# Transposed attention scores as four pairs of 64-row products, with the row maxima in the same shape

## The chip, the cores and the metric

The kernel runs on one core of a Trainium2 chip. The metric is the device time of one execution in microseconds. Before the change it is 2519.74 us (median of three runs, 2518.32 to 2525.74).

The core has a matrix engine (TensorE, PE in the profile, its weight loads listed as PEld), a vector engine (VectorE, DVE), an engine for activations (ScalarE, ACT), a general engine (GpSimd, POOL) and a queue for transfers (SyncE, SP). Operands lie in the on-chip memory of 128 partitions. Products go to PSUM, which has eight banks of 512 float32 per partition here.

## The reference

A two-layer encoder over 1024 tokens of width 1024, in float32. Layer 0 mixes tokens by attention, layer 1 by pooling; each layer then attends to 256 memory tokens and runs a gated network with a width-3 convolution. The change touches layer 0's attention and the start of what follows it. With 16 query heads and 4 key heads of width 64 it computes

```
q = rope(rmsnorm(q)) * 64 ** -0.5 ; k = rope(rmsnorm(k))
scores = einsum('bkgqd,bksd->bkgqs', q, k)      # 1024 x 1024 for each of 16 heads
p = softmax(scores)                             # over the keys
o = einsum('bkgqs,bksd->bkgqd', p, v)
x = x + o @ w_o
```

The gains of the normalisations are large, so the scores are too, and the exponentials need the row maxima taken off first.

## The kernel before

**Precision.** Products run on operands in a reduced float32 form. Each operand is split into a high and a low part, and a product is the sum of high x high, high x low and low x high (lines 759 to 761, the helper for all large products). The high part is made on ScalarE (line 672), the low part on VectorE (line 675).

**Stages.** `attention` has two stages with a planner each. The first (94 to 184 us of it concern this text) makes keys, values and queries from the normalised tokens, tile of 128 tokens by tile, in the order of the list `QKV`. The second is the attention loop, from 183.9 to 544 us. Then `run` multiplies by `w_o`, adds the residual rows `X` and goes on.

**The planner.** A `Plan` collects steps with an engine, an estimated time, what they read and write and which pool of buffers they take from. TensorE's steps keep the order in which they are added. Those of the other engines are ordered by due times, which are worked back from the TensorE steps that need them; `late` sets a due time by hand, so many microseconds behind TensorE's planned clock. `plan.run()` plays this forward and emits the instructions. Outside of the planners the framework orders the instructions. An instruction that waits blocks its engine's queue.

**Layout of q and k.** Queries and keys are kept transposed: the 64 numbers of a head on partitions, tokens along the row. `K[0]` holds the high part of a key head twice, on partitions 0 to 63 and 64 to 127. `K[1]` holds the low part on partitions 0 to 63 and a row of ones on partition 64 (`plan_ones`, line 1133). A block of `Q` holds one query head: its high part on one half of the partitions and its low part on the other, and which half is which changes with the head's parity.

**Groups.** The loop runs over 16 groups, a group being a pair of query heads (x = 0, 1) with one half of the queries (512), and in a group over eight tiles of 128 keys. Two key tiles make a step, four steps a group.

**Scores** (`plan_scores`, lines 1222 and 1224) come transposed, keys on partitions, queries along the row, since the values' product needs them so. For one head and key tile that is a product of 128 rows (high keys with both parts of the queries) and one of 65 (low keys with a copy of the high queries, and the row of ones with a row of negated maxima). The result lies in one PSUM bank (`pT`, three of them), and ScalarE makes its exponential of 512 columns (line 1232) into a half of a tile `pt` (six tiles).

**Maxima** (`peaks`, line 789; `biggest`, line 795) come from the same scores, not transposed and in the high parts alone: queries on partitions, 64 rows, two heads on the two halves of the partitions. The pair fills a tile `pA` of two banks (two such tiles), and one VectorE reduction of 1024 columns gives two columns of `nm`. After eight of them `joined` (line 802) makes eight columns, and `shift` sends them as eight small transfers (line 814) into the row beside the copy of the high queries, which two more transfers bring (line 810). The place of this copy is a ring of four halves of storage slots. The maxima of a group are made during the group before it, and for the first group during the first stage (items `S` of `QKV`).

**Values and sums** (`plan_values`, line 1260; `plan_sum`, line 1293): a step's values product stands one step behind its scores, in full float32, two heads on the two column halves. VectorE adds the two exponentials of each step (line 1267), POOL adds these up over the group (line 1270), and a product with ones sums over the partitions. The sums go by small transfers through a reciprocal (line 1306) and back, POOL scales the result (line 1320), and it is split in high (ScalarE) and low (VectorE) parts for `w_o`.

Of the kernel before, what the change touches and what calls it, by code (L numbers as in the profile page):

```python
# [10 lines left out]
F32 = mybir.dt.float32  # L11
# [32 lines left out]
         for it in ([q, ("S", n // 3)] if n % 3 == 2 else [q])),  # L44
       ("V", 4), ("V", 5), ("V", 6), ("V", 7))
# [588 lines left out]
class Kernel:  # L634
# [140 lines left out]
    def attention(self):  # L775
# [6 lines left out]

        def peaks(G, n, S):

            half, m = GROUPS[G]
            q, t, kh = R.v(Q[m // 2, half], 4), n // 2, n % 2
            for x in range(2):
                rows = slice(x * HD, (x + 1) * HD)
                nc.tensor.matmul(S[:, x * 512:(x + 1) * 512], q[rows, m % 2 * 2 + x, t * P:(t + 1) * P],  # L789
                                 R.v(K[0][kh], 4)[rows, m // 2], start=True, stop=True)  # L790

        def biggest(G, n, S):
            if n == 0:
                NM[G] = self.stat(16, "nm")
            nc.vector.tensor_reduce(NM[G][:, 2 * n:2 * n + 2], S.rearrange("p (x k) -> p x k", x=2), axis=AX.X, op=OP.max,  # L795
                                    negate=True)
# [8 lines left out]
        def shift(G, h):  # L805

            half, m = GROUPS[G]
            q, qm = R.v(Q[m // 2, half], 4), R.hv(h).bitcast(F32)
            for x in range(2):
                nc.sync.dma_start(out=qm[:HD, x * 512:(x + 1) * 512],  # L810
                                  in_=q[x * HD:(x + 1) * HD, m % 2 * 2 + x].bitcast(F32))
            nm = NM.pop(G)
            for i in range(8):
                nc.sync.dma_start(out=qm[HD:HD + 1, i * P:(i + 1) * P], in_=nm[:, i:i + 1].bitcast(F32))  # L814

        with tc.tile_pool(name="qk", bufs=1, reuse_waits="tile") as qk, self.psum("psq", 1, 6) as self.ps:
# [222 lines left out]
            def plan_k(t, b):  # L1039
# [4 lines left out]
                def view(h):  # L1044
                    return R.hv(h)[:, :768].rearrange("p (h i c) -> p h i c", h=4, i=3)
# [5 lines left out]
                def low():  # L1051
                    kst = view(at[half])
                    nc.vector.tensor_tensor(out=kst[:, :, 2], in0=q3(), in1=kst[:, :, 0].bitcast(F32), op=OP.subtract)
                plan.add("copy", 650, high, [qn], [half], [("half", half)], [qn])
                plan.add("add", 350, low, [qn, half], [half], uses=[qn, half])
# [3 lines left out]
            def plan_turn_k(t):  # L1059
                half = ("kst", t)  # L1060
                for i in range(2):
                    b = ("kturned", t, i)

                    def turn(i=i, b=b):
                        kst = R.hv(at[half])[:, :768].rearrange("p (h i c) -> p h i c", h=4, i=3)
                        p = at[b] = self.psB().rearrange("p (a b) -> p a b", a=4)
                        for h in range(4):
                            src = kst[:, h, 2] if i else kst[:, h, :2].rearrange("p a b -> p (a b)")
# [1298 lines left out]
```

## Time and profile before

| what | value |
|---|---|
| median of three runs | 2519.74 us |
| profiled execution | 2520.43 us, its span 2518.7 us |
| PE / PEld / DVE / ACT / POOL busy | 99% / 78% / 77% / 49% / 14% of the span |
| attention loop | 183.9 to 544 us of the span |
| granted clock over the whole span | 0.993 |

A row of a group reads: line, engine, operation, output<-inputs with shapes, xcount | busy us, mean ns of one | idle us of the engine just before, and who ended it. A row of the timeline reads: start in us from the span's start, duration in us, engine, line, operation, xcount of merged instructions, and in brackets the idle time before with its releaser. Ends of products are modelled and overlap with what follows, so starts are the better measure. A granted clock of 1.00 is the full clock of TensorE.

### The profile page before, as it was taken

Reading aid. Unit: us, or ns where it says so; the run is one execution under the profiler, and the core shown is the slowest. Engines: PE = TensorE matmul, PEld = TensorE weight load, DVE = VectorE, ACT = ScalarE, POOL = GpSimd, SP = SyncE. Lnnn points to the kernel's source line nnn. Section 1 sums busy time; section 2 is a strip of 40 time slices with the busy share of each in tenths; the row PEclk is TensorE's granted clock in tenths of the full one; section 3 lists DMA queues with packets and bytes.
Section 4 is the critical chain, followed back from the end, with each engine's and each line's share of the span. In section 5 each row is a group of like instructions: output and inputs, shape, how many; then the busy total and the mean of one; then the engine's idle time right before and its main releaser. Section 6 shows DMA issues by size and latency. Waiting matters only on the chain.

```text
span 2518.7 us, 33712 instructions
## 1 busy us (share of the span) xinstructions
PE 2485.2 (99%) x12302; PEld 1962.5 (78%) x12302; DVE 1936.9 (77%) x2645; ACT 1229.3 (49%) x2070; POOL 355.6 (14%) x407
## 2 busy tenths in 40 slices
PE   9999999999999999999999999999999999999998
PEld 9984434357899888888888888889888888888887
DVE  7887877853886479888879775887559988888875
ACT  6544545542546346554556443655436554554542
POOL 5663433330102000000000002102000000000001
PEclk9998999999999999999999999999999999999999
DMA  4310111142487123432448663289223423337852
GB/s 162 92 26 14 26 26 26 36 145 73 155 299 237 48 80 103 124 105 87 122 145 280 191 215 94 103 280 331 84 76 97 123 86 109 111 103 243 283 193 96
DMA packets 334171, 329.11 MB, mean 131 GB/s; under 512 B 32941, under 2 KB 264733, under 8 KB 334005
## 3 DMA queue, kind: packets, MB, share of 16 engines
q1 hardware_dynamic: 334005, 326.95, 40.7%
q8 instruction: 97, 1.59, 0.3%
q14 instruction: 69, 0.57, 0.1%
HBM read 235.10 MB, written 82.64 MB: 126 GB/s over the span
## 4 chain that ended last, share of the span: by engine, by line
PE 82%; DVE 8%; issue 3%; DMA 3%; SPq 2%; POOL 0%; ACT 0%; POOLq 0%; DVEq 0%; ACTq 0%
PE pB L759 22%; PE pB L761 22%; PE pB L760 22%; PE pA L761 3%; PE pA L759 3%; PE pA L760 3%; DVE nm L795 2%; SPq L814 2%; DVE R L675 2%; DVE scr L1267 2%; PE pO L1260 1%; PE pT L1222 1%; PE pB L328 1%; PE pT L1224 1%; PE pA L789 1%
## 5 line engine op out<-in xcount | busy, mean ns | idle before, releaser
L759 PE MATMUL pB<-R,R 128*128 128x512 f32 (+1 forms) x2732 | 1016.1, 372 | 2.3 <-ACT R L672 0.9
L761 PE MATMUL pB<-R,R 128*128 128x512 f32 (+1 forms) x2728 | 1008.5, 370 | 2.2 <-DVE R L675 2.1
L760 PE MATMUL pB<-R,R 128*128 128x512 f32 (+1 forms) x2732 | 1009.7, 370 | 0.2 <-DVE R L675 0.2
L759 PEld LDWEIGHTS pB<-R,R 128*128 128x128 f32 x2732 | 515.5, 189 | 93.7 <-ACT R L672 2.1
L761 PEld LDWEIGHTS pB<-R,R 128*128 128x128 f32 x2728 | 514.6, 189 | 90.2 <-DVE R L675 3.9
L760 PEld LDWEIGHTS pB<-R,R 128*128 128x128 f32 x2732 | 515.6, 189 | 86.5 <-DVE R L675 1.2
L672 ACT ACTIVATE R<-scr 128x512 fp32r<-128x512 f32 (+3 forms) x376 | 272.9, 753 | 235.8 <-DMA scr<-Gs 59.3
L675 DVE TENSOR_TENSOR R<-scr,R 128x512 fp32r<-128x512 f32 (+3 forms) x364 | 321.4, 911 | 29.7 <-ACT R L672 29.1
L675 DVE TENSOR_TENSOR R<-X,R 128x512 fp32r<-128x512 f32 x374 | 252.1, 685 | 67.5 <-ACT R L672 66.8
L672 ACT ACTIVATE R<-X 128x512 fp32r<-128x512 f32 x374 | 231.8, 630 | 133.7 <-PE pB L760 66.6
L732 POOL TENSOR_SCALAR ms<-ss 128x1 f32<-128x1 f32 (+2 forms) x97 | 31.0, 320 | 1652.2 <-ACT R L740 1282.9
L1232 ACT ACTIVATE pt<-pT 128x512 f32<-128x512 f32 x256 | 148.8, 599 | 151.3 <-PE pT L1224 149.6
L442 ACT COPY scr<-pB 128x512 f32<-128x512 f32 x156 | 91.0, 584 | 180.3 <-PE pB L761 173.2
L795 DVE TENSOR_REDUCE nm<-pA 128x2 f32<-128x1024 f32 x128 | 150.6, 1211 | 27.7 <-PE pA L789 27.6
L1942 DVE TENSOR_TENSOR X<-pB,X 128x512 f32<-128x512 f32 (+1 forms) x145 | 99.3, 686 | 82.5 <-PE pB L761 81.2
L759 PE MATMUL pA<-R,R 128*128 128x512 f32 (+1 forms) x420 | 150.7, 359 | 0.0
L761 PE MATMUL pA<-R,R 128*128 128x512 f32 (+1 forms) x420 | 150.3, 358 | 0.0
L760 PE MATMUL pA<-R,R 128*128 128x512 f32 (+1 forms) x420 | 150.0, 357 | 0.0
L1270 POOL TENSOR_TENSOR scr<-scr 128x1024 f32<-128x1024 f32 x46 | 115.2, 2504 | 191.9 <-DVE scr L1267 191.9
L1260 PE MATMUL pO<-pt,V 128*64 128x512 f32 x512 | 127.1, 619 | 0.0
L1222 PE MATMUL pT<-R,R 128*128 128x512 f32 x256 | 121.9, 476 | 0.0
L1222 PEld LDWEIGHTS pT<-R,R 128*128 128x128 f32 x256 | 48.7, 190 | 85.9 <-issue 53.5
(182 smaller groups left out, 3065.1 us busy)
## 6 DMA issues: line engine op xcount, KB each, us to landing
X<-in_ffn_w_up SPq DMA_DIRECT2D x82, 512.0 KB
Gs<-X SPq DMA_DIRECT2D x105, 256.0 KB
scr<-in_ffn_w_down SPq DMA_DIRECT2D x45, 512.0 KB
scr<-Gs SPq DMA_DIRECT2D x35, 512.0 KB
scr<-in_xattn_w_kv SPq DMA_DIRECT2D x32, 512.0 KB
scr<-Gs SPq DMA_DIRECT2D x42, 384.0 KB
scr<-in_attn_w_qkv SPq DMA_DIRECT2D x22, 512.0 KB
Wt<-scr SPq DMA_DIRECT2D x44, 256.0 KB
```

What stands on the lines that cost most here:

```text
L442: self.nc.scalar.copy(out, p)
L672: self.nc.scalar.activation(hi, src, AF.Copy)
L675: self.nc.vector.tensor_tensor(out=lo, in0=src, in1=hi.bitcast(F32), op=OP.subtract)
L759: mm(out, ah, bh, start=start, stop=False)
L760: mm(out, ah, bl, start=False, stop=False)
L761: mm(out, al, bh, start=False, stop=stop)
L795: nc.vector.tensor_reduce(NM[G][:, 2 * n:2 * n + 2], S.rearrange("p (x k) -> p x k", x=2), axis=AX.X, op=OP.max, negate=True)
L1222: nc.tensor.matmul(T[b], R.v(K[0][kt // 4], 4)[:, m // 2, cols], R.v(Q[m // 2, half], 4)[:, m % 2 * 2 + x], start=True, stop=False)
L1232: nc.scalar.activation(E[G, kt][:, x * 512:(x + 1) * 512], T.pop(b), AF.Exp)
L1260: nc.tensor.matmul(O[G][x * HD:(x + 1) * HD], V32[:, kt, m // 2], E[G, kt][:, x * 512:(x + 1) * 512], start=kt == 0, stop=kt == NT - 1)
L1270: nc.gpsimd.tensor_tensor(out=acc[G, 0], in0=acc[G, 0], in1=acc.pop((G, d)), op=OP.add)
L1942: nc.vector.tensor_tensor(out=x, in0=banks[b][:, c], in1=x, op=OP.add)
```

## The change

Layout: a block of `Q` now holds one part of two query heads, one on each half of the partitions; the next block holds the other part. `K[1]` holds the low part of a key head on both halves, made by a fourth column block in the staging of the keys. Queries are no longer copied for the shift.

Scores: a key tile of both heads goes into one PSUM tile of two banks (two such tiles), as four pairs of 64-row products, the two heads on the two halves: high keys with high queries, high keys with low queries, low keys with high queries, and a block `one` (zeros, and ones on partitions 0 and 64) with a block that holds the negated maxima on partitions 0 and 64. The last pair is a step of its own, which alone waits for the shift. One exponential covers both heads. The blocks of the shift lie in one slot, zeroed once in the first stage; `shift` sends the eight small transfers alone.

Maxima: the two heads go to single banks (`pS`, three, which the column sums share) and are reduced apart, 512 columns each. Ahead of and behind the scores of a step stands one pair of maxima, and in the first four steps a third between them. In the first stage the last two pairs stand among the last values products, and the last reduction, the join and the transfers get due times.

POOL: of a group's four steps the last is not added on VectorE but by two POOL additions that read the exponentials. The low parts of the result are made on POOL.

Residual rows: the six tiles `pt` are placed first in their pool, and the tiles `X` are placed in the order 1, 3, 0, 2, 4, 6, 5, 7 over them and what follows.

```diff
-         for it in ([q, ("S", n // 3)] if n % 3 == 2 else [q])),
-       ("V", 4), ("V", 5), ("V", 6), ("V", 7))
+         for it in ([q, ("S", n // 4)] if n % 4 == 1 else [q])),
+       ("S", 6), ("V", 4), ("S", 7), ("V", 5), ("V", 6), ("V", 7))
...
+        def rows(x):
+            return slice(x * HD, (x + 1) * HD)
...
-                rows = slice(x * HD, (x + 1) * HD)
-                nc.tensor.matmul(S[:, x * 512:(x + 1) * 512], q[rows, m % 2 * 2 + x, t * P:(t + 1) * P],
-                                 R.v(K[0][kh], 4)[rows, m // 2], start=True, stop=True)
+                nc.tensor.matmul(S[x], q[rows(x), m % 2 * 2, t * P:(t + 1) * P], R.v(K[0][kh], 4)[rows(x), m // 2],
+                                 start=True, stop=True)
...
-        def shift(G, h):
...
-            for x in range(2):
-                nc.sync.dma_start(out=qm[:HD, x * 512:(x + 1) * 512],
-                                  in_=q[x * HD:(x + 1) * HD, m % 2 * 2 + x].bitcast(F32))
-            nm = NM.pop(G)
+        def shift(G, ring):
+
+            to, nm = self.R.hv((ring, G % 4 // 2)).bitcast(F32)[:, G % 2 * 512:(G % 2 + 1) * 512], NM.pop(G)
             for i in range(8):
-                nc.sync.dma_start(out=qm[HD:HD + 1, i * P:(i + 1) * P], in_=nm[:, i:i + 1].bitcast(F32))
+                nc.sync.dma_start(out=to[i // 4 * HD:i // 4 * HD + 1, i % 4 * P:(i % 4 + 1) * P], in_=nm[:, i:i + 1].bitcast(F32))
+
+        one = self.cst.tile([P, P], F32R, name="unit")
+
+        def constant(out, value, p=slice(0, P)):
+            n = out.shape[1] // P
+            nc.gpsimd.tensor_scalar(out[p].rearrange("p (a b) -> p a b", b=P),
+                                    self.ident[p, None, :].to_broadcast([p.stop - p.start, n, P]), 0.0, value, op0=OP.mult, op1=OP.add)
...
-                    nc.vector.tensor_tensor(out=kst[:, :, 2], in0=q3(), in1=kst[:, :, 0].bitcast(F32), op=OP.subtract)
+                    nc.vector.tensor_tensor(out=kst[:, :, 2:], in0=q3()[:, :, None, :].to_broadcast([P, 4, 2, HD]),
+                                            in1=kst[:, :, :2].bitcast(F32), op=OP.subtract)
...
-                plan.add("tap", 1024, lambda: biggest(0, n, at.pop(b)), [b], [("nm", n)], uses=[b])
...
+                plan.add("tap", 1024, lambda: biggest(0, n, at.pop(b).rearrange("p (x k) -> p x k", x=2)), [b], [("nm", n)],
+                         uses=[b], late=3.0 if n == 7 else 9.0)
...
+            first = [at.tile([P, 1024], F32, name="pt", bufs=6) for _ in range(6)]
...
-            plan = Plan(R, {}, {"A": 2, "B": 3, "O": 1, "pt": 6, "scr": 6, "qm": 3, "half": len(R.freed)})
+            plan = Plan(R, {}, {"A": 3, "B": 2, "O": 1, "pt": 6, "scr": 6, "qm": 3, "half": len(R.freed)})
...
+                def emit(first):
+                    if first:
+                        T[b] = self.ps.tile([P, 1024], F32, name="pT", bufs=2)
+                    q, k = R.v(Q[m // 2, half], 4), [R.v(K[i][kt // 4], 4) for i in range(2)]
+                    mr = R.hv((ring, G % 4 // 2))[:, G % 2 * 512:(G % 2 + 1) * 512]
+                    for i, j in ((0, 0), (0, 1), (1, 0)) if first else ((2, 0),):
+                        for x in range(2):
+                            left = k[i][rows(x), m // 2, cols] if i < 2 else one[rows(x)]
+                            right = q[rows(x), m % 2 * 2 + j] if i < 2 else mr[rows(x)]
+                            nc.tensor.matmul(T[b][:, x * 512:(x + 1) * 512], left, right, start=(i, j) == (0, 0), stop=i == 2)
...
+                def exp():
+                    E[G, kt] = at.tile([P, 1024], F32, name="pt", bufs=6)
+                    nc.scalar.activation(E[G, kt], T.pop(b), AF.Exp)
+                plan.add("product", 3, partial(emit, True), (), [b], [("B", b)])
+                plan.add("product", 1, partial(emit, False), [("qm", G)], [(b, 1)], (), [("qm", G)], gives=("half", 2) if done else None)
...
+                u, mine = ("acc", G, 0), d < 3 or G == last
...
+                for kt in ks if not mine else ():
+                    plan.add("pool", 900, partial(more, lambda kt=kt: E[G, kt]), [u, ("E", G, kt)], [u], uses=[u, ("pt", G, kt)], late=5.0)
...
-                    self.low(h, l, src) if lo else self.high(h, src)
+                    if lo:
+                        nc.gpsimd.tensor_tensor(out=l, in0=src, in1=h.bitcast(F32), op=OP.subtract)
...
-                    plan_scores(G, 0, 2 * d)
-                    plan_scores(G, 1, 2 * d)
...
+                    peak()
+                    plan_scores(G, 2 * d)
+                    if n < 4:
+                        peak()
+                    plan_scores(G, 2 * d + 1)
+                    peak()
...
-        X = [xp.tile([P, D], F32, name=f"X{t}") for t in range(NT)]
+        X = {t: xp.tile([P, D], F32, name=f"X{t}") for t in (1, 3, 0, 2, 4, 6, 5, 7)}
+        X = [X[t] for t in range(NT)]
```

133 lines of the change are left out of this document (60 added, 73 removed).

## The prediction, made before the result was known

> **What bounds the kernel now.** First the page: busy shares and the chain that ended last.
>
> ```profile
> PE 2485.2 (99%) x12302; PEld 1962.5 (78%) x12302; DVE 1936.9 (77%) x2645; ACT 1229.3 (49%) x2070; POOL 355.6 (14%) x407
> PE 82%; DVE 8%; issue 3%; DMA 3%; SPq 2%; POOL 0%; ACT 0%; POOLq 0%; DVEq 0%; ACTq 0%
> ```
>
> TensorE sets the end nearly everywhere, so the change is worth what it saves of TensorE's time in the attention loop, as long as nobody else gets in the way. Then the busy times by stretch: start of the loop, steady loop, whole loop (first product of maxima at 183.9 to first product of the output projection at 544), and what follows.
>
> ```profile
> core 0: us, PE busy (x) PEld busy (x) DVE busy (x) ACT busy (x) POOL busy (x), PEclk, DMA share, GB/s
> 183.90:206.00 22.10, 18.70 (x48) 7.96 (x48) 10.05 (x10) 6.59 (x12) 3.90 (x2) 0.69 0.03 1
> 206.00:537.80 331.80, 328.10 (x1263) 133.10 (x1262) 262.72 (x236) 167.82 (x305) 133.32 (x60) 0.99 0.13 30
> 183.90:544.00 360.10, 353.00 (x1337) 143.03 (x1337) 274.85 (x247) 176.22 (x320) 137.22 (x62) 0.98 0.12 28
> 544.00:600.00 56.00, 49.91 (x226) 41.36 (x227) 20.07 (x26) 16.67 (x29) 5.86 (x8) 0.94 0.45 160
> ```
>
> TensorE is busy in 328.1 of 331.8 us of the steady loop, but weight loads take only 133: in this stage its busy time hides gaps. The timeline of TensorE over one step (two key tiles of a pair of heads) shows them.
>
> ```profile
> 305.62 0.50 PE L1222 MATMUL pT<-R,R 128*128 128x512 f32 x1
> 305.96 0.40 PE L1224 MATMUL pT<-R,R 65*128 65x512 f32 x1
> 306.19 0.40 PE L1222 MATMUL pT<-R,R 128*128 128x512 f32 x1
> 306.42 0.39 PE L1224 MATMUL pT<-R,R 65*128 65x512 f32 x1
> 306.74 0.51 PE L789 MATMUL pA<-R,R 64*128 64x512 f32 x2
> 307.18 0.50 PE L1222 MATMUL pT<-R,R 128*128 128x512 f32 x1
> 307.52 0.40 PE L1224 MATMUL pT<-R,R 65*128 65x512 f32 x1
> 307.85 0.49 PE L789 MATMUL pA<-R,R 64*128 64x512 f32 x2
> 308.27 0.50 PE L1222 MATMUL pT<-R,R 128*128 128x512 f32 x1
> 308.61 0.40 PE L1224 MATMUL pT<-R,R 65*128 65x512 f32 x1
> 308.94 1.94 PE L1260 MATMUL pO<-pt,V 128*64 128x512 f32 x8
> 310.81 0.50 PE L1222 MATMUL pT<-R,R 128*128 128x512 f32 x1
> ```
>
> Read the starts. Inside a run of score products one follows the other after 0.23 us (305.96, 306.19, 306.42). The first of a run takes 0.34 until the next, the last 0.32 until another shape begins. Each run of one shape so costs 0.11 + 0.09 = 0.20 us beside its products. A pair of maxima products (two heads, 64 rows each, running at once) stands alone and takes 0.43, of which 0.23 is its product. The step is 5.19 us and has five such runs ahead of its values.
>
> **The change part by part.**
>
> *Scores of 64 rows.* A score tile of one head is now two products (128 and 65 rows), so a key tile of both heads takes four. After, it takes four pairs of 64-row products, two heads at once. How many there are:
>
> ```profile
> L1222 PE MATMUL pT<-R,R 128*128 128x512 f32 x256 | 121.9, 476 | 0.0
> L1224 PE MATMUL pT<-R,R 65*128 65x512 f32 x256 | 104.4, 408 | 7.1 <-DMA R<-nmr 6.4 <-issue 0.5
> L789 PE MATMUL pA<-R,R 64*128 64x512 f32 x240 | 61.1, 505 | 0.5 <-DVE R L675 0.5
> ```
>
> 512 score products become 512 pairs, the 120 pairs of maxima stay: 632 slots before and after, if a pair streams like one full product. What goes are the switches: maxima and scores now have one shape, and a step is one run of ten pairs and one of values. Each pair of maxima loses its own 0.20 and the 0.20 of the score run that it cut in two: 120 x 0.40 = 48 us. The step becomes 5.19 - 0.80 = 4.39.
>
> That pairs stream is the price most in doubt. The loop's start has the only two in a row:
>
> ```profile
> 183.91 0.73 PE L789 MATMUL pA<-R,R 64*128 64x512 f32 x4 [0.50 <-DVE R L675]
> 183.91 0.30 PEld L789 LDWEIGHTS pA<-R,R 64*128 64x128 f32 x4 [0.74 <-DVE R L675]
> 186.59 0.47 PE L1224 MATMUL pT<-R,R 65*128 65x512 f32 x1 [1.52 <-DMA R<-nmr]
> 189.16 0.76 PE L1224 MATMUL pT<-R,R 65*128 65x512 f32 x1 [1.87 <-DMA R<-nmr]
> ```
>
> One pair lasts 0.51, two last 0.73: the second adds 0.22, and its weights were in by 184.21, while the first still streamed (to 184.42). The ends are 0.22 and, if each pair paid what a lone one pays, 0.43; I take 0.23, since the row of two is the same shape. The page "TensorE: Matmul & The Clock Gate" of the Trainium skill (section "Part 3: Packing small matmuls — row/col tiling") says that a weight load overlaps with products in flight only where the row groups differ; by that each of ten pairs that fill both halves would pay its load, and the sum would be the 2580 us of the second rival below instead of 2466. The loads of 183.91 disagree: they fit the other case that the same section names, a load into the background buffer.
>
> *Start of the loop.* TensorE waits 1.52 and 1.87 us for the shift, and the clock over 22.1 us is 0.69, so another 22.1 x 0.31 = 6.9 us are lost: 10.3 together. Why the shift is late:
>
> ```profile
> 169.73 0.49 PE L789 MATMUL pA<-R,R 64*128 64x512 f32 x2
> 180.33 1.21 DVE L795 TENSOR_REDUCE nm<-pA 128x2 f32<-128x1024 f32 x1
> 181.57 0.62 DVE L802 TENSOR_TENSOR nmr<-nm 128x8 fp32r<-128x8 f32 x1
> ```
>
> The last maxima lay 10.6 us until VectorE took them; from the joined maxima (182.19) to the second product (189.16) the eight small DMAs took 7.0. The change puts this last pair one V product later, but gives its reduction, join and DMAs due times of 3.0 to 4.0 us behind it. With three V products still to come the shift lands about when the first shift pair wants it. I take the 10.3 as gone; ends: all gone, none gone.
>
> *VectorE.* A reduction of 1024 becomes two of 512 (PSUM banks go singly, three of them); one of four additions per group and the two subtractions of the result go to POOL.
>
> ```profile
> L795 DVE TENSOR_REDUCE nm<-pA 128x2 f32<-128x1024 f32 x113 | 132.5, 1210 | 15.6 <-PE pA L789 15.6
> L1267 DVE TENSOR_TENSOR scr<-pt 128x1024 f32<-128x1024 f32 x62 | 79.1, 1278 | 3.2 <-ACT pt L1232 3.0
> L1306 DVE RECIPROCAL rs<-rs 8x128 f32<-8x128 f32 x14 | 13.2, 941 | 47.4 <-DMA rs<-scr 47.4
> L681 DVE TENSOR_TENSOR R<-pB,R 128x512 fp32r<-128x512 f32 x6 | 3.9, 685 | 2.7 <-ACT R L680 2.7
> L1270 POOL TENSOR_TENSOR scr<-scr 128x1024 f32<-128x1024 f32 x46 | 115.2, 2504 | 191.9 <-DVE scr L1267 191.9
> L1320 POOL TENSOR_TENSOR scr<-scr 128x512 f32<-128x512 f32 x14 | 18.2, 1297 | 21.3 <-DMA scr<-inv 19.4 <-DMA R<-R 1.9
> ```
>
> A 512-wide reduction lies between 0.605 (half of 1.21) and 0.685 (the nearest 512-wide row); I take 0.65. Per group of four steps: 16 x 0.65 + 3 x 1.28 + 0.94 + 0.2 = 15.4 us. A group of four steps will last 4 x 4.39 and a column sum, some 18.5 us. VectorE fits with 83%, against 79% now, and stays hidden on average. In the first four steps three pairs of maxima come per step (six reductions and an addition, 5.2 us, against 4.6 of TensorE, and in the first step 3.9 against 2.7): about 3 us of waiting. PSUM gives cover there: a pair needs the first reduction of the pair before it.
>
> *POOL and ACT.* POOL per group: 4 x 2.50 + 1.30 + two subtractions of 256 at 0.65 or so (half of 1.30) = 12.6 of 18.5 us. Two of its additions now read the exponentials themselves and so hold their tiles; the six tiles come round after three steps (13 us), and POOL's four additions (10 us) begin a step before the tiles of the last two are written, so they are out in time. ACT, busy for 167.8 of 331.8 us, does one exponential of 1024 instead of two of 512, so no more than now. Both stay hidden; if POOL falls 3 us behind, the exponentials wait for tiles.
>
> *SP and DMAs.* Per group two copies of queries go, the eight small ones stay.
>
> ```profile
> L810 SPq DMA_DIRECT2D R<-R x32: 461/592/600, 166.8 to 514.4; - x32
> ```
>
> SP issues 32 x 0.59 = 19 us less, hidden at a DMA share of 0.13. The wait for the shift now stands before the fourth pair of a key tile, with all later products of TensorE queued behind it. Maxima end two whole steps ahead (1.9 + 2 x 4.4 + 1.2 = 11.9 us) of it, against a chain of two reductions (1.3), the join and 7.0: some 9. The 3 us that L1224 waited after the start (6.4 - 3.4) may go; I leave them.
>
> *Projections.* Eight low parts of the keys grow from 256 to 512 wide (at most 8 x 0.35 = 2.7 us of VectorE), POOL swaps two rows of ones for two zero fills. TensorE, busy for 99% of the span, covers both. But the last two pairs of maxima share one PSUM buffer and now stand one V product apart: TensorE can wait for a reduction there, 0 to 7 us (before, one lay 10.6; a V product is 2.8). By the due times I take 1.
>
> *Residual rows.* Only addresses change: the first loads can come free before the last values.
>
> ```profile
> 572.08 1.97 PE L328 MATMUL pB<-ident,X 128*128 128x128 f32 x8 [6.09 <-DVE X L323]
> L323 DVE SCALAR_TENSOR_TENSOR X<-X,rs,scr 128x1024 f32<-128x1024 f32 x3 | 3.9, 1284 | 13.0 <-DMA Xq<-X 10.8 <-POOL rs L734 2.2
> ```
>
> There TensorE idles 6.09 us since the saving of the first row tile queues among the loads, and a clock of 0.94 costs 56 x 0.06 = 3.4 more: 9.5 to gain if the loads come sooner. If they come ahead of the second half of the output weights, some 5 to lose. SP works in order, and these loads stood behind the last group's normaliser; I take 0.
>
> *Sum.* -48 - 10.3 + 3 + 1 = -54.3 us. The profiled execution took 2520.43 us (span 2518.7), 0.7 above the median of 2519.74; 2520.4 - 54.3 = 2466.
>
> **The rivals.**
>
> 1. *VectorE becomes the bound* (chance 0.12). An addition on VectorE stalls behind a running POOL one:
>
> ```profile
> 355.42 2.94 DVE L675 TENSOR_TENSOR R<-scr,R 128x256 fp32r<-128x256 f32 x2
> 355.57 2.50 POOL L1270 TENSOR_TENSOR scr<-scr 128x1024 f32<-128x1024 f32 x1 [1.65 <-DVE scr L1267]
> ```
>
> Two subtractions took 2.94 us, the second until POOL was done at 358.07. With POOL busy 12.6 of 18.5 us (0.68), three additions a group could each wait 0.68 x 2.5 = 1.7. With reductions at 0.685 that makes 16 x 0.685 + 3 x (1.28 + 1.7) + 1.1 = 21.0 us a group, 2.5 above TensorE's: 16 x 2.5 = 40 less gained, 2506; with half of these stalls it is 18.5, and nothing is lost. I price it between, 2486. It decides from 18.5 us a group. Against: POOL's additions follow VectorE's by themselves, so few should meet.
>
> 2. *Pairs do not stream: slower* (0.09). If each pair's weights load only after the pair before, a pair costs the 0.43 of a lone one, 632 x 0.20 = 126 us more than at 0.23; the 64 x 0.20 = 13 of the steps' own run are then counted in: 2466 + 126 - 13 = 2579, some 2580. It decides from 0.23 + 54 / 632 = 0.32 us a pair. Against: 0.73 for two. For: accumulation over four pairs into two banks at once is shown nowhere.
>
> 3. *The 0.20 is no switch but semaphores* (0.05), which stay: gain only at the start, 2520 - 10.3 + 4 = 2514. Against: it shows at every change of shape and nowhere inside a run.
>
> 4. *The residual rows come early as well* (0.12): 2466 - 9.5 = 2456.
>
> **How the numbers follow.** My forecast has 0.62. The measurement can tell about 0.3%, 7.6 us. Rivals 1 and 4 are faster too, rival 3 half of it: faster 0.88, same 0.03, slower 0.09. The range goes from everything gained (waits of 3 us and 9.5 as well, 3 and 1 not paid: 2449) to rival 1 with the start's loss unmended (2486 + 10, and 4 for waits: 2500); the likeliest case alone, 2452 to 2480.
>
> **What would show it.** Right: runs of ten 64-row pairs every 0.23 us, a step near 4.4, the loop near 306 us instead of 360, the start's clock at 1.0, no copies of queries. Wrong: pairs 0.3 or more apart; VectorE without idle time and products waiting for reductions; additions of several us beside POOL; a wait for the shift at each group.

## The result and the profile after

The changed kernel takes 2456.57 us (median of four, 2455.41 to 2459.45) against 2520.06 for the kernel before on the same chip: a ratio of 0.9746, with an interval of 0.9728 to 0.9763. The forecast was 2466, in a range of 2449 to 2500. The profiled execution took 2456.54 us, its span 2454.7. Its page still names TensorE as the bound; its share of the chain that ended last has risen from 82% to 88%. The page's rows of busy time and of the chain's shares:

```profile
PE 2428.4 (99%) x12814; PEld 1970.4 (80%) x12814; DVE 1914.2 (78%) x2718; ACT 1211.7 (49%) x1942; POOL 428.3 (17%) x457
PE 88%; DVE 4%; issue 3%; POOL 2%; DMA 1%; ACT 1%; SPq 0%; POOLq 0%; DVEq 0%; ACTq 0%
```

Busy times by stretch, in the columns of the table before: start of the loop, steady loop, whole loop (from about the first product of maxima to the first of the output projection), and the 56 us behind it.

```profile
184.60:206.00 21.40, 20.96 (x134) 12.09 (x136) 20.15 (x34) 10.23 (x11) 9.30 (x5) 1.00 0.03 1
206.00:474.00 268.00, 267.51 (x1675) 136.83 (x1672) 224.94 (x290) 144.97 (x179) 194.65 (x101) 1.00 0.11 23
184.30:482.40 298.10, 296.48 (x1849) 151.80 (x1847) 249.18 (x325) 158.79 (x193) 204.86 (x105) 1.00 0.10 23
482.40:538.50 56.10, 50.71 (x227) 42.01 (x228) 19.79 (x22) 16.24 (x28) 8.29 (x13) 0.94 0.43 158
```

The loop lasts 298.3 us (184.09 to 482.37) instead of 360.0 (183.91 to 543.93), so 61.7 of the 63.9 us between the two profiled executions come from it. The first columns say what became tight: VectorE is busy for 84% of the steady loop (224.9 of 268) and POOL for 73% (before, 79% and 40%). The last row has not changed: the clock is 0.94 there as before.

One step in TensorE's timeline:

```profile
299.78 0.50 PE L791 MATMUL pS<-R,R 64*128 64x512 f32 x2
300.12 0.87 PE L1234 MATMUL pT<-R,R 64*128 64x512 f32 x6
300.82 0.40 PE L1234 MATMUL pT<-R,unit 64*128 64x512 f32 x2
301.06 0.85 PE L1234 MATMUL pT<-R,R 64*128 64x512 f32 x6
301.75 0.39 PE L1234 MATMUL pT<-R,unit 64*128 64x512 f32 x2
301.98 0.40 PE L791 MATMUL pS<-R,R 64*128 64x512 f32 x2
302.31 1.94 PE L1272 MATMUL pO<-pt,V 128*64 128x512 f32 x8
304.17 0.50 PE L791 MATMUL pS<-R,R 64*128 64x512 f32 x2
```

From 299.78 to 304.17 are 4.39 us. The run of ten pairs takes 2.53: three pairs of scores start at 300.12 and the fourth at 300.82, which is 0.70 for three, 0.23 each. Only the run's first pair (0.34) and its last (0.33) cost more.

The start of the loop, where TensorE waited 1.52 and 1.87 us for the shift:

```profile
184.84 0.97 PE L1234 MATMUL pT<-R,R 64*128 64x512 f32 x6 [0.24 <-ACT R L1110]
185.65 0.40 PE L1234 MATMUL pT<-R,unit 64*128 64x512 f32 x2
```

The first shift pair (185.65) follows its scores at once, and the clock of this stretch is 1.00 instead of 0.69. The groups of VectorE and POOL in the loop:

```profile
L797 DVE TENSOR_REDUCE nm<-pS 128x1 f32<-128x512 f32 x240 | 153.5, 684 | 38.8 <-PE pS L791 38.1
L1281 DVE TENSOR_TENSOR scr<-pt 128x1024 f32<-128x1024 f32 x49 | 73.0, 1492 | 2.6 <-ACT pt L1240 2.6
L803 DVE TENSOR_TENSOR nmr<-nm 128x8 fp32r<-128x8 f32 x15 | 9.0, 597 | 0.5
L1284 POOL TENSOR_TENSOR scr<-scr,pt 128x1024 f32<-128x1024 f32 x30 | 73.1, 2437 | 2.6 <-ACT pt L1240 0.3
```

A reduction of 512 takes 0.684 us, at the upper end of what was estimated. VectorE's additions have grown from 1.278 to 1.492 and its join from 0.172 to 0.597, with no change of their own, while POOL's share rose (its own additions take 2.44). VectorE's idle time in front of reductions (38.8 us) says that it still waits for TensorE, not the other way: in the steady loop TensorE's products wait for reductions for 0.5 us in all.

### The profile page after: what moved, and what is told of

Same layout as the page of the kernel before. It is cut to its first block, busy times and chain, and to the rows that moved or that the text cites. A ratio compares the mean times of both kernels' runs of the same rounds, so it can differ in the third digit from the quotient of the medians.

```text
span 2454.7 us, 34706 instructions
## 1 busy us (share of the span) xinstructions
PE 2428.4 (99%) x12814; PEld 1970.4 (80%) x12814; DVE 1914.2 (78%) x2718; ACT 1211.7 (49%) x1942; POOL 428.3 (17%) x457
## 3 DMA queue, kind: packets, MB, share of 16 engines
q8 instruction: 101, 1.65, 0.3%
## 4 chain that ended last, share of the span: by engine, by line
PE 88%; DVE 4%; issue 3%; POOL 2%; DMA 1%; ACT 1%; SPq 0%; POOLq 0%; DVEq 0%; ACTq 0%
PE pB L759 21%; PE pB L761 21%; PE pB L760 21%; PE pT L1234 5%; PE pO L1272 5%; PE pA L761 3%; PE pA L759 3%; PE pA L760 3%; PE pS L791 2%; POOL rs L734 1%; PE pB L328 1%; DVE R L675 1%; PE pS L1308 1%; POOL qn L1032 1%; DVE nm L797 0%
## 5 line engine op out<-in xcount | busy, mean ns | idle before, releaser
L675 DVE TENSOR_TENSOR R<-scr,R 128x512 fp32r<-128x512 f32 (+2 forms) x332 | 282.6, 879 | 26.8 <-ACT R L672 26.4
L797 DVE TENSOR_REDUCE nm<-pS 128x1 f32<-128x512 f32 x240 | 153.5, 684 | 38.8 <-PE pS L791 38.1
L1240 ACT ACTIVATE pt<-pT 128x1024 f32<-128x1024 f32 x128 | 127.1, 1024 | 88.1 <-PE pT L1234 86.0
L444 DVE TENSOR_TENSOR scr<-pB,scr 128x512 f32<-128x512 f32 x156 | 107.0, 686 | 11.3 <-PE pB L761 11.0
L1234 PE MATMUL pT<-R,R 64*128 64x512 f32 x768 | 111.9, 393 | 0.2 <-ACT R L1110 0.2
L1806 DVE SCALAR_TENSOR_TENSOR scr<-scr,conv 128x1023 f32<-128x1023 f32 x66 | 84.6, 1282 | 20.8 <-ACT scr L1801 18.9
```

Of the source, the lines that this page charges most:

```text
L444: self.nc.vector.tensor_tensor(out=out, in0=p, in1=out, op=OP.add)
L675: self.nc.vector.tensor_tensor(out=lo, in0=src, in1=hi.bitcast(F32), op=OP.subtract)
L797: nc.vector.tensor_reduce(NM[G][:, 2 * n + x.start:2 * n + x.stop], S, axis=AX.X, op=OP.max, negate=True)
L1234: nc.tensor.matmul(T[b][:, x * 512:(x + 1) * 512], left, right, start=(i, j) == (0, 0), stop=i == 2)
L1240: nc.scalar.activation(E[G, kt], T.pop(b), AF.Exp)
```

## The experiments

Each kernel was timed beside the kernel before on one chip. Loop means from the first product of maxima to the first of the output projection, in the profiled execution; steps are counted between the starts of their values.

| kernel | median us | ratio to before (interval) | loop us | plain step us |
|---|---|---|---|---|
| before | 2520.06 | | 360.0 | 5.19 |
| changed | 2456.57 | 0.9746 (0.9728 to 0.9763) | 298.3 | 4.38 |
| e1_gathered | 2496.42 | 0.9907 (0.9892 to 0.9922) | 334.6 | 4.62 |
| e2_split | 2477.51 | 0.9833 (0.9817 to 0.9849) | 319.7 | 4.74 |
| e3_nodue | 2459.68 | 0.9766 (0.9751 to 0.9780) | 303.3 | 4.38 |
| e4_vector | 2470.51 | 0.9806 (0.9792 to 0.9821) | 309.9 | 4.37 |
| e5_xorder | 2458.58 | 0.9752 (0.9736 to 0.9768) | 298.3 | 4.38 |
| e6_due_before | 2511.34 | 0.9964 (0.9952 to 0.9976) | 351.4 | 5.19 |
| e7_loads | 2451.17 | 0.9727 (0.9713 to 0.9742) | 298.2 | 4.38 |
| e8_runs | 2490.15 | 0.9880 (0.9866 to 0.9895) | 330.3 | joined |
| e9_ahead | 2511.36 | 0.9963 (0.9952 to 0.9974) | 350.9 | 5.19 |
| e10_copies | 2458.67 | 0.9758 (0.9743 to 0.9772) | 298.2 | 4.38 |
| e11_joined | 2457.63 | 0.9757 (0.9740 to 0.9773) | 305.0 | joined |

### Is it the change of shape? e1_gathered and e2_split

The first takes the kernel before, with its layout and its products, and only puts the maxima of a step together.

```diff
+                    ahead = [((n + 5) // 4, (n + 5) % 4 * 2 + i) for i in range(2)]
+                    if ahead[0][0] <= last:
+                        plan_peaks(*ahead[0])
+                        plan_peaks(*ahead[1])
                     plan_scores(G, 0, 2 * d)
                     plan_scores(G, 1, 2 * d)
-                    ahead = [((n + 5) // 4, (n + 5) % 4 * 2 + i) for i in range(2)]
-                    if ahead[0][0] <= last:
-                        plan_peaks(*ahead[0])
                     plan_scores(G, 0, 2 * d + 1)
-                    if ahead[0][0] <= last:
-                        plan_peaks(*ahead[1])
                     plan_scores(G, 1, 2 * d + 1)
```

> The kernel before with both pairs of maxima of a step ahead of its eight score products, all operands and shapes as before. Theory (a change of product shape costs 0.20 us beside the products, whatever the layout): the step has two runs of products ahead of its values instead of five, so 3 x 0.20 = 0.60 us less in each of the 60 steps with maxima, 36 us, and some 2484 us; the step 4.6 us instead of 5.19. Rival (the 0.20 are waits for buffers and semaphores, which go with the products wherever they stand): the step stays at 5.2 us, 2520 us. Second rival (the three score banks or the two maxima tiles run out when the products stand closer): a step between the two with TensorE waiting for ScalarE or VectorE, and 2495 to 2510 us.

From TensorE's timeline of e1_gathered, first the maxima of a step with a column sum, then the start of the next step, a plain one:

```profile
302.25 0.50 PE L789 MATMUL pA<-R,R 64*128 64x512 f32 x2
303.00 0.49 PE L789 MATMUL pA<-R,R 64*128 64x512 f32 x2 [0.25 <-ACT scr L1297]
```

```profile
307.37 0.73 PE L789 MATMUL pA<-R,R 64*128 64x512 f32 x4
308.04 0.51 PE L1222 MATMUL pT<-R,R 128*128 128x512 f32 x1
```

The two pairs of maxima now take 0.67 together (307.37 to 308.04) instead of 0.86 apart, and the eight score products run through to the values at 310.18. Plain steps are 4.62 us, against the 4.6 of the theory, so more than a third of the whole gain comes by moving two lines, without any product of 64 rows in the scores. (Of the 25 us that its loop is shorter some 3.5 are the clock at the loop's start, 0.85 over 183.9 to 206 instead of 0.69.) The end was less good than forecast (2496 instead of 2484): steps with a column sum take 6.0 instead of the 5.5 that 6.06 less three changes of shape would be, as the second pair of maxima then waits for ScalarE to empty a bank (303.00), and near the end there is one wait of 5.7 us. That is the second rival, in part.

The second goes the other way: it takes the changed kernel and cuts its values in two.

```diff
...
                     plan_scores(G, 2 * d)
                     if n < 4:
                         peak()
+                    if n:
+                        plan_values(*steps[n - 1], 0)
                     plan_scores(G, 2 * d + 1)
                     peak()
                     if n:
-                        plan_values(*steps[n - 1])
+                        plan_values(*steps[n - 1], 1)
...
```

> The changed kernel with the values products of a step split in two, one half between the two key tiles. Same products, same count. Theory: a step has four runs instead of two, 2 x 0.20 us more in each of 64 steps, 26 us: step 4.8, some 2482 us. Rival (the gaps are waits): nothing new is waited for, since the exponentials of the step before are long made: 2457 us, within 4.

TensorE's timeline of e2_split:

```profile
302.79 0.50 PE L791 MATMUL pS<-R,R 64*128 64x512 f32 x2
303.12 0.86 PE L1234 MATMUL pT<-R,R 64*128 64x512 f32 x6
303.82 0.39 PE L1234 MATMUL pT<-R,unit 64*128 64x512 f32 x2
304.14 1.08 PE L1272 MATMUL pO<-pt,V 128*64 128x512 f32 x4
305.15 0.97 PE L1234 MATMUL pT<-R,R 64*128 64x512 f32 x6
...
307.52 0.50 PE L791 MATMUL pS<-R,R 64*128 64x512 f32 x2
```

Nothing waits, yet the step is 4.73 us (302.79 to 307.52) instead of 4.39: 0.34 for two more runs, 0.17 each, and 21 us over the loop. The same price appears with no new wait and disappears with no wait removed, so it belongs to the change of shape. (In e2_split the number format changes along with the shape, as the values are in full float32; in e1_gathered the shape alone does.) That the engine drains at such a change is what the Trainium skill says ("TensorEngine Tiling (Array Packing)", section "Key Properties"); the runs give the price, 0.17 to 0.20 us here.

### What cured the start? e3_nodue and e6_due_before

The changed kernel without the due times by hand, and the kernel before with them alone:

```diff
-                         uses=[b], late=3.0 if n == 7 else 9.0)
+                         uses=[b])
...
-                    plan.add("load", 3, lambda: shift(0, sets[1][0]), ["nm", ("zero", 0)], [("zero", 0)], late=4.0)
+                    plan.add("load", 3, lambda: shift(0, sets[1][0]), ["nm", ("zero", 0)], [("zero", 0)])
```

> The changed kernel without the due times set by hand in the first stage (last reduction, join, zero fills, ones, shift of the first group). Theory (the due times cure the late shift): the last maxima lie some 10 us again and start one V product later than before, so TensorE waits 3 to 8 us at the loop's start and the clock drops there to about 0.7: 10 to 15 us more, 2467 to 2472. Rival (it is the two copies, the rows of ones and the new order that cure it): 2457 within 3, clock 1.0 at the start.

```diff
-                plan.add("tap", 1024, lambda: biggest(0, n, at.pop(b)), [b], [("nm", n)], uses=[b])
+                plan.add("tap", 1024, lambda: biggest(0, n, at.pop(b)), [b], [("nm", n)], uses=[b],
+                         late=3.0 if n == 7 else 9.0)
...
-                plan.add("load", 1, lambda: shift(0, (sets[1][0], 0)), ["nm"], [("w", 1, 0), ("w", 1, 1)])
+                plan.add("load", 1, lambda: shift(0, (sets[1][0], 0)), ["nm"], [("w", 1, 0), ("w", 1, 1)], late=4.0)
```

> The kernel before with the due times of the first stage alone (last reduction 3.0, others 9.0, join 3.5, shift 4.0 us). Theory (the shift of the first group is late since the last maxima lie 10.6 us): the reduction follows within some 3 us, the shift lands before the loop, TensorE's waits of 1.5 and 1.9 us and the clock of 0.69 go: 8 to 10 us less, 2510. Rival (something else holds it, the copies of queries or the fill of the ones among POOL's work): 2517 to 2523 with both waits still there.

The start in TensorE's timeline of e3_nodue, and the busy times of its first 16 us:

```profile
184.64 0.46 PE L1234 MATMUL pT<-R,unit 64*128 64x512 f32 x1 [0.27 <-DMA R<-nmr]
187.12 0.76 PE L1234 MATMUL pT<-R,unit 64*128 64x512 f32 x1 [2.02 <-DMA R<-nmr]
```

```profile
184.00:200.00 16.00, 13.36 (x74) 8.43 (x72) 10.73 (x18) 5.81 (x6) 3.52 (x2) 0.79 0.02 1
```

The timeline of e6_due_before at the same place, and the busy times of its start:

```profile
183.31 0.50 PE L1223 MATMUL pT<-R,R 128*128 128x512 f32 x1
183.64 0.40 PE L1225 MATMUL pT<-R,R 65*128 65x512 f32 x1
```

```profile
182.60:206.00 23.40, 23.35 (x92) 10.36 (x94) 20.37 (x18) 11.35 (x21) 11.51 (x5) 1.00 0.08 12
```

In the kernel before, the due times alone remove both waits and bring the clock to 1.00: 8.6 us of the loop, 0.9964 (0.9952 to 0.9976). In the changed kernel their absence brings the wait back, but it is 5.0 us of the loop, less than the 10 to 15 expected. The second wait is 2.02 us and the clock costs less: a mean of 0.79 over 16 us is 6.7 us at half speed, where 0.69 over 22.1 us had been 13.7. Three pairs of scores go ahead of the first shift pair now, so there is more to do while the shift is under way; that this is why the clock costs less is not shown. Whole executions of e3_nodue and the changed kernel are not told apart by their intervals.

### Room on VectorE: e4_vector

```diff
-                u, mine = ("acc", G, 0), d < 3 or G == last
+                u, mine = ("acc", G, 0), True
...
-                        nc.gpsimd.tensor_tensor(out=l, in0=src, in1=h.bitcast(F32), op=OP.subtract)
+                        self.low(h, l, src)
...
```

> The changed kernel with the fourth addition of each group and the low parts of the result back on VectorE. Theory (moving them is needed, as VectorE is close to the bound): VectorE is busy 249 of 298 us in the loop now, 15.6 us of a group's 18.4; an addition of 1.2 to 1.5 and two low parts of 0.4 to 1.4 bring 2.0 to 4.3 us, so 17.6 to 19.9 of 18.4, and TensorE waits for reductions: 5 to 25 us more, 2462 to 2482. Rival (there was room enough): 2457 within 3.

Busy times in the steady loop of e4_vector, and its group of additions:

```profile
206.00:480.00 274.00, 267.64 (x1642) 136.14 (x1640) 255.21 (x329) 141.29 (x173) 130.70 (x57) 1.00 0.10 23
```

```profile
L1281 DVE TENSOR_TENSOR scr<-pt 128x1024 f32<-128x1024 f32 x58 | 104.9, 1808 | 0.9 <-ACT pt L1240 0.9
```

VectorE is busy for 93% now, its additions take 1.81 us, and every fourth step takes 5.15 instead of 4.38: the loop is 11.6 us longer. TensorE falls behind well before VectorE is full. So the first rival of the prediction, VectorE as the bound, was near: without the move to POOL it decides a part of the steps.

### Where the residual tiles lie, and when they are loaded: e5_xorder and e7_loads

```diff
-        X = {t: xp.tile([P, D], F32, name=f"X{t}") for t in (1, 3, 0, 2, 4, 6, 5, 7)}
-        X = [X[t] for t in range(NT)]
+        X = [xp.tile([P, D], F32, name=f"X{t}") for t in range(NT)]
```

> The changed kernel with the residual tiles placed in the order 0 to 7 again (the exponentials' tiles still first). Theory (the placement moves nothing, since the first residual load stands behind the last group's normaliser on SP and starts 9 us after the loop in both kernels): 2457 within 3, TensorE's idle time ahead of the first transposes 5 to 6 us. Rival (the placement gave part of the gain beyond the forecast): 2459 to 2465, the loads later or the idle time longer.

2458.58 us and an idle time of 5.9 us ahead of the transposes: no difference that the intervals show, as the theory has it. The new places of the residual tiles did nothing by themselves that can be told. What does is the order of the loads:

```diff
-        for t in range(NT):
-            ...
-            nc.sync.dma_start(out=X[t], in_=a["x"][0][t * P:(t + 1) * P, :])
+        def fetch(*ts):
+            for t in ts:
+                nc.sync.dma_start(out=X[t], in_=a["x"][0][t * P:(t + 1) * P, :])
+        ws.append(self.load_rows(a["attn_w_o"][0], 1))
+        fetch(0, 2)
+        behind = {(1, 2): (4, 6), (0, 4): (1, 3), (1, 4): (5, 7)}
...
+        def late(n, t):
+            fetch(*behind.pop((n, t), ()))
+            product(n, t)
...
```

> The changed kernel with two residual loads ahead of the output projection and the other six behind its third to fifth product rows. Theory (TensorE idles 5.4 us behind the loop since the saving of the first row tile queues among eight loads of 512 KB, and the clock then drops for 6.8 us): the saving lands within 3 us, the idle time shrinks to about 1 us and the drop goes, 4.4 + 3.4 = 7.8 us less, some 2449. Rival (the idle time is the chain of norm and transposes itself): 2457 within 3.

The transposes behind the loop in the timeline of the changed kernel, then in that of e7_loads, and the busy times of the 56 us behind the loop in e7_loads:

```profile
509.84 1.54 PE L328 MATMUL pB<-ident,X 128*128 128x128 f32 x6 [5.39 <-DVE X L323]
```

```profile
505.43 1.09 PE L328 MATMUL pB<-ident,X 128*128 128x128 f32 x8 [0.89 <-DVE X L323]
```

```profile
482.40:538.50 56.10, 55.16 (x258) 45.64 (x259) 22.72 (x26) 18.23 (x32) 8.85 (x14) 1.00 0.46 163
```

With six of the eight loads behind the first saved row tiles (and the second half of the output weights ahead of all eight) VectorE's longest wait for a saved tile falls from 7.2 to 2.8 us, TensorE's idle time from 5.39 to 0.89 us and the clock of the stretch from 0.94 back to 1.00. In the medians that is 5.4 us, of 7.8 expected; the two ratios' intervals still overlap a little (0.9742 and 0.9728). This is the fastest kernel of the study: 2451.17 us.

### Why the groups' first steps got faster: e9_ahead and e10_copies

In the kernel before the first steps of groups 3 to 14 (counted from 0) took 5.3 to 5.9 us instead of 5.19. In the changed one they take 4.4 like the others, which the forecast had not counted on. Two things could have done it: the maxima end earlier, or the copies of queries are gone. The last group, too, began late: two rows of the kernel before, a wait for the shift in its first step and the values that follow.

```profile
520.89 0.47 PE L1224 MATMUL pT<-R,R 65*128 65x512 f32 x1 [1.01 <-DMA R<-nmr]
523.42 3.55 PE L1260 MATMUL pO<-pt,V 128*64 128x512 f32 x8
```

Elsewhere these eight products take 1.94 us; here the clock over 523.5 to 527.1 is 0.53. To tell the two causes apart, earlier maxima go into the kernel before (with the due times), and the copies go back into the changed kernel:

```diff
-                for i in range(2):
+                for i in range(4):
                     plan_peaks(1, i)
...
-                    ahead = [((n + 5) // 4, (n + 5) % 4 * 2 + i) for i in range(2)]
+                    ahead = [((n + 6) // 4, (n + 6) % 4 * 2 + i) for i in range(2)]
...
```

> The kernel before with the due times and, beside them, each group's maxima half a step's work further ahead (two more pairs made before the loop, so a group's last pair stands one whole step earlier). Theory (the 0.1 to 0.8 us that the first step of each group takes over 5.19 are waits for the shift, as the maxima end too late for its chain of some 9 us): the first steps fall to 5.2 and 5 to 7 us go against the due times alone (2511): 2505. Rival (the two copies of queries on SP and the DMA queues make the shift late): the first steps stay at 5.3 to 6.0, 2511 within 3.

```diff
+            if G:
+                half, m = GROUPS[G]
+                q, there = R.v(Q[m // 2, half], 4), R.hv((sets[1][1], G % 2)).bitcast(F32)
+                for x in range(2):
+                    nc.sync.dma_start(out=there[:HD, x * 512:(x + 1) * 512],
+                                      in_=q[x * HD:(x + 1) * HD, m % 2 * 2].bitcast(F32))
...
```

> The changed kernel with the two copies of queries per group sent again, into a slot that nobody reads. Theory (SP and the DMAs are covered, since the maxima end two steps ahead): 2457 within 3, no wait for the shift at the groups' first steps. Rival (the copies were what made the shift late): first steps of 4.6 to 5.2 instead of 4.4, 5 to 10 us more.

The steady loop in the busy times of e6_due_before, then the loop's start in the timeline of e9_ahead, start and steady loop in its busy times, and the steady loop of e10_copies:

```profile
206.00:528.00 322.00, 317.31 (x1222) 128.93 (x1220) 252.47 (x228) 163.24 (x297) 125.75 (x58) 0.99 0.13 30
```

```profile
185.93 0.50 PE L789 MATMUL pA<-R,R 64*128 64x512 f32 x2 [1.09 <-DVE nm L795]
187.06 0.80 PE L789 MATMUL pA<-R,R 64*128 64x512 f32 x2 [0.63 <-DVE nm L795]
```

```profile
184.00:206.00 22.00, 20.17 (x52) 9.15 (x52) 12.20 (x14) 6.70 (x12) 4.01 (x2) 0.61 0.03 1
206.00:530.00 324.00, 324.00 (x1264) 133.09 (x1264) 237.01 (x233) 166.59 (x307) 134.41 (x60) 1.00 0.13 30
```

```profile
206.00:474.00 268.00, 267.51 (x1678) 137.25 (x1676) 222.70 (x290) 145.30 (x178) 194.12 (x101) 1.00 0.16 36
```

With the maxima a step earlier TensorE has no idle time left in 324 us, and the first steps of these groups are 5.19. The last group gains too. It makes no maxima, so a step is 3.95 us there, and its first two take 5.84 and 5.57 in e6_due_before but 4.20 and 3.94 here. The copies cost nothing: with them the loop is 298.2 us. So the earlier maxima did it. The whole of e9_ahead is no faster than the due times alone, since the four pairs of maxima ahead of its loop give the gain back at once: TensorE waits 1.09 and 0.63 us for reductions there, and the clock of that stretch is 0.61.

### Fewer changes of shape still: e8_runs and e11_joined

```diff
-                    if n:
-                        plan_values(*steps[n - 1])
+                    if n % 2:
+                        if n > 1:
+                            plan_values(*steps[n - 2])
+                        plan_values(*steps[n - 1])
...
```

> The changed kernel with two steps joined: scores and maxima of both in one run, then the values of the two steps before the last. Theory (every change of shape costs 0.18 to 0.20): 32 times two changes fewer, 12 us less, some 2445; steps by twos 8.4 instead of 8.75. Rival (PSUM, the six exponential tiles or ScalarE hold it up: four key tiles come 1.17 us apart, an exponential takes 1.02, and six tiles are all in use): TensorE waits as much as it saves or more, 2457 to 2475.

Busy times of e8_runs in its steady loop, and rows of its view of waits for the same stretch (us in total, times, longest):

```profile
220.00:480.00 260.00, 236.79 (x1456) 123.93 (x1452) 183.66 (x266) 123.98 (x153) 154.23 (x87) 1.00 0.09 20
```

```profile
PEld pS L791 <- DVE nm L797: 24.8, 25, 1.2
PEld pO L1272 <- ACT scr L1294: 19.3, 12, 1.6
PE pS L791 <- DVE nm L797: 14.2, 25, 0.8
```

This lost: TensorE is idle for 23 of 260 us, although VectorE is busy for only 71%. It waits for reductions (two pairs of maxima stand together in the run, with three banks) and for the bank of the results, since the values of two groups now stand in one run. (A weight load and its product wait at the same time, so these rows do not add up.) The second attempt puts the maxima apart again and keeps the values of two groups out of one run:

```diff
                     peak()
                     plan_scores(G, 2 * d)
-                    if n < 4:
-                        peak()
+                    peak()
                     plan_scores(G, 2 * d + 1)
-                    peak()
-                    if n:
-                        plan_values(*steps[n - 1])
+                    for _ in range(2 if n == 0 else n < 5):
+                        peak()
+                    if n and n % 2 == 0:
+                        plan_values(*steps[n - 2])
+                        plan_values(*steps[n - 1])
...
```

> The changed kernel with the late residual loads, and with steps joined by twos once more, in the pairing that keeps the values of two steps in one group (so one bank of results does), a pair of maxima ahead of each key tile instead of two together, and groups of maxima a step and a half further ahead. Theory (what held the first joining up was the bank of the results and two pairs of maxima in a row, each 1.37 us of VectorE): 8.4 us for two steps against 8.76, 2451 - 12 + 4 for the start = 2443. Rival (VectorE, busy for 84% already, cannot take a run of 4.7 us with 5.5 us of reductions whatever the order, or the six tiles of exponentials bind): two steps at 8.8 to 10, 2451 to 2485.

Better, but the loop is 305.0 us against 298.2 in e7_loads, which it is built on. The best two steps take 8.6 us (9.5 with a column sum), hardly less than two of 4.38, and others up to 10.7, one near the end 12.4. So here the saving of a change of shape is eaten when the run in between grows. Which of VectorE's order, ScalarE's pace and the six tiles binds in e11_joined wasn't separated.

## Why the prediction was right, point by point

- **632 slots and 0.23 us a pair.** Right: 0.23 in the after timeline, in every run of ten. The weight loads of six such products take 0.66 us, from 299.88, and lie under products on the same two halves of the partitions. The sentence of the page "TensorE: Matmul & The Clock Gate" of the Trainium skill that loads overlap only where the row groups differ is at odds with these rows; the background buffer, which the same section names, would fit them. The slower rival fell with the 0.23.
- **48 us by the switches.** Right in mechanism and size: plain steps 5.19 to 4.38, forecast 4.39; e1_gathered and e2_split show it from both sides, at 0.17 to 0.20 each. The third rival (semaphores) fell.
- **10.3 us at the start.** Right: the waits and the low clock are gone. The due times are the cause in the kernel before (8.6 us of the loop); in the new order of products they are worth 5.0 of it.
- **3 us of waiting in the first steps.** About right. Up to the first values the loop has 22 pairs, 5.3 us with the ends of the run, and took 7.0 (184.09 to 191.07); the next two steps took 4.76 and 4.94 us where 4.62 is a step with a third pair of maxima, and one soon after took 5.21. That makes 3.0 us.
- **"The 3 us that L1224 waited after the start may go; I leave them."** This is the term that was mis-sized, and the reason why the loop took 298.3 us instead of the 305 of the sum. They went, and there were more than 3. In the kernel before the first steps of twelve groups exceed 5.19 by 4.8 us together (5.9 in e6_due_before). The first two steps of the last group take 5.91 and 5.59 us instead of 3.95, which is 2.0 us of waiting and 1.6 us of clock. Together these are 8.4 us, more than the 6.4 by which the loop beat its sum; where the other 2 went was not separated. The idle column counts only what is left when the modelled end of the product before has passed, and products of 0.4 us that start every 0.23 hide the first part of each wait. The starts show it.
- **VectorE, POOL.** The 0.65 us of a reduction was 0.684 and additions grew to 1.49, but VectorE stayed below TensorE (84% in place of 83%). e4_vector shows how near the first rival was.
- **Copies of queries and residual rows at nothing.** Right (e10_copies, e5_xorder). The idle time behind the loop was 6.09 and is 5.39; the fourth rival, the rows coming early, did not happen by the placement, and e7_loads shows what it takes.
- **1 us in the projections.** The loop starts at 184.09 instead of 183.91: nothing, within what can be told.

By the terms: forecast -54.3, profiled executions -63.9. The loop gave 61.7 instead of the 55.3 that the sum had for it; the remaining 2.2 lie behind and ahead of the loop, where kernels with the same code differ by more (the part behind the loop took 1972 to 1978 us in the changed kernel, e2_split, e3_nodue, e4_vector and e5_xorder).

## What to carry to other kernels

Read TensorE's timeline by starts, not by busy time: here 99% busy hid 0.17 to 0.20 us at every change between 128-row, 64-row and column-half products, and putting products of one shape together was worth about a third of the gain with no other edit. Half-height pairs cost one full product if they stream in a row, so a layout that brings all of a stage's products into one shape can pay even at the same number of slots. Joining runs further did not pay here: in e8_runs TensorE waited for the reductions and the copy that empty PSUM, and in e11_joined, where a longer run lost more than it saved as well, what bound stayed open.

## What the runs showed that was not expected

A short wait can cost more in clock than in waiting. In e9_ahead two waits of 1.09 and 0.63 us at the loop's start stand ahead of a stretch with a granted clock of 0.61 over 22 us (8.6 us lost); in e3_nodue one of 2.02 us goes with 6.7 us at half speed; while 0.89 us in e7_loads left it at 1.00. (In the slow stretch of the kernel before, score products start 0.43 us apart, at 193.04 and 193.47, instead of 0.23: about half speed.) The drop goes with waits, but what exactly sets its length, 6.7 us in one and 17 us (0.39 x 22 / 0.5) in the other, stays open. The length of the waits alone doesn't: e1_gathered has the same two waits of 1.09 and 0.63 us at its start, and a third of 0.92, and its clock there is 0.85.

VectorE's small join grew from 0.172 to 0.597 us and its additions from 1.278 to 1.492, without any change of their own, when POOL's share of the loop rose from 40% to 73%; yet in e4_vector, with POOL at 48%, the additions took 1.808. So POOL's share doesn't explain it. What counts is whether the instructions of the two engines meet: first a join and an addition of the changed kernel, then an addition of e4_vector, each behind a POOL instruction that has begun before it.

```profile
303.65 2.48 POOL L1343 TENSOR_TENSOR R<-scr,R 128x256 fp32r<-128x256 f32 x2 [1.56 <-ACT R L672]
303.73 0.67 DVE L803 TENSOR_TENSOR nmr<-nm 128x8 fp32r<-128x8 f32 x1
306.09 2.37 POOL L1284 TENSOR_TENSOR scr<-scr 128x1024 f32<-128x1024 f32 x1
308.00 1.55 DVE L1281 TENSOR_TENSOR scr<-pt 128x1024 f32<-128x1024 f32 x1
```

```profile
300.56 2.38 POOL L1284 TENSOR_TENSOR scr<-scr 128x1024 f32<-128x1024 f32 x1 [3.64 <-DVE scr L1281]
301.54 2.48 DVE L1281 TENSOR_TENSOR scr<-pt 128x1024 f32<-128x1024 f32 x1
```

Both additions end 1.1 us after POOL's has ended (308.46 and 302.94), and 1.21 us is what an addition takes that meets no POOL instruction. In the steady loop of the changed kernel 13 of 14 joins meet one and take 0.66 on average, the other takes 0.172; the additions that meet one take 1.65 on average. In e4_vector it is 2.36: POOL's addition still has 1.40 us to run where VectorE's begins in these rows, against 0.46 in the changed kernel. Reductions, which read PSUM, take 0.684 either way. The Trainium skill ("SBUF — State Buffer", section "Who interferes with whom") says that a VectorE instruction with two inputs in SBUF and a POOL instruction that reads SBUF contend, over a pair of ports that is an exclusive lock. The trace agrees: what grew is of that kind, by about the time that POOL's instruction still had to run. What to ask of work on POOL is thus not how much it is but beside what it falls.
